# A hybrid decoder step on one core: order of the first loads, place of the tables, rows of tiles 1 to 3 ahead of the queries' weights, and the maximum of those weights on DVE

## The chip, the core and the metric

The kernel runs on one core of a Trainium2 chip. The metric is the device time of one execution in microseconds, the median of several. The core's engines each work through their own instructions in order: PE (matrix products, with PEld for loading the stationary operand), DVE (vector), ACT (activation), POOL (general), and SP, whose queue issues nearly all DMAs here. They wait for each other through semaphores.

## What is computed

One step of a one-layer decoder for 2048 prompt rows and 64 sample rows (8 sequences of 8 new tokens):

```python
h = rmsnorm(x, norm_w)
z = h @ w_in                                   # 1024 -> 3600 columns
q, k, v, qb, kb, vb, g_lr, gate_a, gate_b = jnp.split(z, split_points(), axis=-1)
q = rope(rmsnorm(heads(q, H_A), q_norm_w), pos)
k = rope(rmsnorm(heads(k, H_A), k_norm_w), pos)
o_a = attend(q, k, v)                          # mixture of three dilated windows
o_b, s_fin = gla_chunked(qb * DK_B**-0.5, kb, vb, log_a, s0)
o_b = rmsnorm(o_b, gla_norm_w)
mixed = concat([o_a * silu(gate_a), o_b * silu(gate_b)])
y = x + mixed @ w_out
```

The attention mixes windows of 128, 512 and 2048 rows with strides of 1, 4 and 16. The sample rows attend to cached keys and values in the same way. The outputs are y for prompt and sample, the last keys and values, and the states of the linear attention.

## The kernel before

**Numbers as pairs.** Every fp32 operand of the large products is split into two fp16 parts, a high one and what it leaves, after scaling by a power of two; a product is then three fp16 products (high by high, high by low, low by high). ACT writes the high part, DVE the low one. This holds for the rows x and for the weights.

**Rows.** The 2048 prompt rows are 16 tiles of 128; the sample rows are a tile of 64, called "s". `fetch` (L490) loads a tile of x, `prep` (L505) treats it: a sum of squares on ACT (L520), an inverse root in small steps on ACT and DVE (`rsqrt`, L117), the scaled high part on ACT (L528), the low part on DVE (L529), then a transposing DMA on SP (L532) into `hl`, and a store of `hl` to `h_d` (L536) for later projections. The sample tile is transposed on PE instead (L543). Tiles 0 to 3 have buffers of their own (`early`, `early_ht`).

**Weights.** `load_w` (L579) is a generator for one block of columns (v, q, k and others): eight DMAs of 128 x 512 into `raws` (L591), a maximum over the block, a scale from it, and eight splits into fp16 parts (ACT L635, DVE L636). The pool of raw buffers, `wr`, has four pairs, just one block, so the next block's loads wait until splits have released pairs. For v the maximum is exact: DVE reduces the absolute values row by row (L603). For the others ACT sums squares (L608), and two more ACT steps take the root of the largest sum (L622, L623). In both ways `spread_max` (L566) has PE turn the column of maxima (L569), DVE reduce it (L571) and PE spread the result to all partitions (L572). The scale of the columns is then `ns` (L630).

**Projections.** `project` (L1085) multiplies one tile by one block: 24 matmuls for a full tile (L1105), 16 for the sample tile (L779), into one of two PSUM buffers (`ps_Y`). `post` (L708) takes the result out: for v, ACT writes the fp32 values to a staging buffer of which there are two (L736, tag "z2"), stored by SP (L737, for the sample tile also L739), then ACT and DVE write the fp16 parts (L744, L745). For q and k, `qk_take` and `qk_post` normalize and rotate on ACT, POOL and DVE.

**Order.** The program text gives priorities, and a planner, which runs a simulated timeline, decides the order of the instructions on each engine and in SP's queue before anything runs. On the chip every engine and SP's queue keep that order, also where the first of them has to wait. The text begins (L995 to L999) with the load of the sample tile, the whole of `load_w("v")`, in which x of tile 0 goes between the fourth and the fifth load and tiles 1 to 3 behind the eighth, and then `prep` of the sample tile and tiles 0 to 3. There follow small tables: `nwo`, four loads of single columns (L1004), the attention masks `m3w` and `m3c`, the norm tables `tabs` with their power-of-two scales `scl` (L1017 to L1044). Then `first(0)` (L1124) projects v for "s" and tiles 0 to 3, q for 0 to 3, k for 0 to 3; `load_w("q")` is called behind v of tile 0, `load_w("k")` behind v of tile 3. `first(1)` to `first(3)` treat four tiles each, woven with attention work. `sample_keys` (L956) loads cached keys for the sample rows' scores; its loads need no result of the program.

## Time and profile before

| | |
|---|---|
| median of three runs | 1355.9 us (1350.35, 1355.9, 1356.49) |
| profiled execution | 1347.42 us, its span 1345.6 us |
| mean granted clock of PE | 0.979 |
| DMA | 285.27 MB, mean 212 GB/s |
| first matmul of v, tile 0 | 25.46 us |
| first matmul of q, tile 0 | 59.59 us |
| first matmul of k, tile 0 | 85.19 us |

Times in the profile count from the start of the span. A row of the timeline has the start, the length, the engine, the line of the kernel, the operation and its operands, and how many instructions were merged; in brackets stands the time for which the engine had been idle, and what ended that wait. "SPq" is SP's queue of DMA issues; the length there is that of the issue and not of the transfer. A row of the view by lines groups all instructions of a line with the same operands: busy time and mean length of one, then the idle time ahead of them.

### The profile page before, as it was taken

What the parts mean: (1) busy time and instruction counts of PE and PEld (TensorE: products, weight loads), DVE (VectorE), ACT (ScalarE), POOL (GpSimd) and SP (SyncE); (2) the same over time, 40 slices, a digit from 0 to 9 for tenths busy, and PEclk for the clock granted to TensorE, in tenths of its full rate; (3) what the DMA queues carried; (4) which work ended last, traced back from release to release, by engine and by line L of the source; (5) the groups of instructions that cost most, each with busy time, mean ns of one, the idle gap of its engine ahead of it and who ended that gap; (6) DMA issues with size and microseconds to landing.
All of it is one profiled execution on the core that took longest, in us unless ns stands there. A gap on an engine that the chain in (4) does not pass through costs nothing.

```text
span 1345.6 us, 26148 instructions
## 1 busy us (share of the span) xinstructions
PE 1218.3 (91%) x8878; PEld 722.5 (54%) x8878; DVE 933.1 (69%) x2266; ACT 878.8 (65%) x2331; POOL 641.6 (48%) x597
## 2 busy tenths in 40 slices
PE   3798999988899798998999998789999999999998
PEld 1343565555566555665766565556655544444443
DVE  6367767788677968767771769977564387787842
ACT  5655787778568877788994557655776475465520
POOL 0076554878678645651115756777440033332310
PEclk9999999999999999999999998989999999999999
DMA  8859857778957599969886355455335768998952
GB/s 259 243 162 260 233 162 161 203 203 216 238 167 207 174 278 274 299 183 220 215 190 196 85 165 199 144 168 157 98 111 190 275 197 302 376 325 312 351 200 83
DMA packets 251721, 285.27 MB, mean 212 GB/s; under 512 B 125426, under 2 KB 160195, under 8 KB 251587
## 3 DMA queue, kind: packets, MB, share of 16 engines
q1 hardware_dynamic: 251586, 283.60, 70.7%
q8 instruction: 70, 1.15, 0.4%
q14 instruction: 65, 0.52, 0.1%
HBM read 183.12 MB, written 75.24 MB: 192 GB/s over the span
## 4 chain that ended last, share of the span: by engine, by line
PE 35%; DVE 20%; DMA 17%; POOL 10%; issue 9%; ACT 6%; SPq 3%; POOLq 0%; DVEq 0%; ACTq 0%
PE Y L1579 5%; DVE qbd L243 3%; PE acc_vb L1105 3%; PE acc_qkb L1105 3%; POOL pr L951 3%; PE acc_gb L1105 3%; PE O L467 2%; PE acc_g L1105 2%; PE s L434 2%; PE t L452 2%; DMA v<-vp_d 2%; DMA qb<-q_d 2%; PE acc_q L1105 2%; PE acc_k L1105 2%; POOL pt L419 2%
## 5 line engine op out<-in xcount | busy, mean ns | idle before, releaser
L1105 PEld LDWEIGHTS <-hr 128*128 128x128 f16 x1824 | 174.5, 99 | 133.1 <-issue 21.6
L951 POOL TENSOR_TENSOR pr<-k,qb 128x512 f32<-128x512 f32 x128 | 176.5, 1379 | 115.8 <-DVE sck L952 79.7
L445 ACT ACTIVATE p<-p,o 128x256 f32<-128x256 f32 (+1 forms) x384 | 173.2, 455 | 53.3 <-DVE o L442 49.4
L1105 PEld LDWEIGHTS <-hl 128*128 128x128 f16 x1248 | 122.4, 100 | 152.3 <-issue 26.2
L1579 PE MATMUL Y<-w_o,mh 128*128 128x512 f16 x768 | 177.5, 381 | 3.5 <-ACT mh L1538 3.4
L419 POOL TENSOR_TENSOR pt<-p,pt 128x512 f16<-128x512 f32 (+1 forms) x80 | 94.4, 1180 | 145.7 <-ACT pt L418 126.1
L1621 POOL TENSOR_TENSOR tc<-oc,w 128x512 f32<-128x512 f32 x32 | 49.0, 1550 | 178.7 <-DVE w L1613 169.5
L467 PE MATMUL O<-v,pt 128*128 128x128 f16 x1200 | 110.3, 220 | 25.1 <-DMA v<-vp_d 7.9
L1579 PEld LDWEIGHTS <-mh 128*128 128x128 f16 x768 | 71.9, 98 | 91.4 <-issue 8.8
L952 DVE TENSOR_REDUCE sck<-pr 128x8 f32<-128x512 f32 x128 | 87.0, 680 | 48.9 <-POOL pr L951 48.5
L452 PE MATMUL t<-ident,p 128*128 128x128 f32 x600 | 105.4, 279 | 5.0 <-ACT p L445 3.0
L467 PEld LDWEIGHTS <-pt 128*128 128x128 f16 x1200 | 81.9, 98 | 51.8 <-POOL pt L419 12.0
L1105 PE MATMUL acc_v<-w_v,hl 128*128 128x512 f16 x384 | 95.2, 391 | 8.5 <-DVE vp L745 3.5
L442 DVE CUSTOM_DVE_ANT_0 p<-s,m3w,scl_s 128x128 f32<-128x128 f32 (+1 forms) x256 | 89.0, 394 | 17.2 <-POOL pt L419 6.0
L1105 PE MATMUL acc_g<-w_g,hr 128*128 128x272 f16 (+1 forms) x768 | 99.2, 277 | 0.0
L1105 PE MATMUL acc_vb<-w_vb,hr 128*128 128x512 f16 x384 | 96.3, 397 | 1.4 <-ACT zg L719 1.4
L1105 PE MATMUL acc_q<-w_q,hl 128*128 128x512 f16 x384 | 93.1, 392 | 4.1 <-ACT zs_k L663 3.4
L235 ACT ACTIVATE E<-D_e 128x256 f32<-128x256 f32 (+1 forms) x168 | 67.8, 418 | 44.4 <-DVE qbd L243 16.9
L1105 PE MATMUL acc_k<-w_k,hl 128*128 128x512 f16 x384 | 91.2, 383 | 2.1 <-ACT zs_k L663 1.6
L1105 PE MATMUL acc_gb<-w_gb,hr 128*128 128x512 f16 x384 | 88.4, 385 | 3.0 <-ACT zgb L728 3.0
L434 PE MATMUL s<-kk,qq 128*128 128x256 f16 (+1 forms) x512 | 79.6, 269 | 9.5 <-DMA kk<-kp_d 4.8
L227 POOL TENSOR_TENSOR D_e<-b_e 128x512 f32<-128x512 f32 x56 | 66.4, 1196 | 23.2 <-ACT E L235 11.0
(508 smaller groups left out, 2598.2 us busy)
## 6 DMA issues: line engine op xcount, KB each, us to landing
k<-in_cache_k_win SPq DMA_DIRECT2D x104, 256.0 KB
sv<-in_cache_v_win SPq DMA_DIRECT2D x24, 1024.0 KB
hr<-h_d SPq DMA_DIRECT2D x44, 512.0 KB
qb<-q_d SPq DMA_DIRECT2D x64, 256.0 KB
o_d<-o SPq DMA_DIRECT2D x96, 132.0 KB
oc<-o_d SPq DMA_DIRECT2D x48, 264.0 KB
x<-in_x_prompt SPq DMA_DIRECT2D x16, 512.0 KB
h_d<-hl SPq DMA_DIRECT2D x16, 512.0 KB
```

Of the source, the lines that this page charges most:

```text
L227: POOL.tensor_tensor(dv, bv, bv[:, :, 0:1, B - 1 : B].to_broadcast([P, M, 2, B]), ALU.subtract)
L235: ACT.activation(ev[rows, i], dv[rows, :, half, :], AF.Exp, scale=(2 * half - 1) / 16.0)
L419: POOL.tensor_tensor(l, f, h, ALU.subtract)
L434: PE.matmul(s_ps[:, i * w : (i + 1) * w], q, k, start=(n == 0), stop=(n == len(prods) - 1),)
L442: DVE.tensor_tensor_reduce(s[:, sl], s_ps[:, sl], mask, neg, BIG, ALU.add, ALU.min, nmf(i))
L445: ACT.activation(s[:, sl], s[:, sl], AF.Exp, bias=nmf(i), scale=-1.0, accum_out=denf(i))
L452: PE.transpose(p_ps[:, i * P : (i + 1) * P], t["s"][:, i * P : (i + 1) * P], ident[:])
L467: PE.matmul(o_, t["pt"][:, c, (i * nb + b) * P : (i * nb + b + 1) * P], vf(i, b), start=(n == 0), stop=(n == 2 * nb - 1),)
L951: POOL.tensor_tensor(pr[:], kt, qt, ALU.mult)
L952: DVE.tensor_reduce(out, pr[:].rearrange("p (u k d) -> p u k d", u=2, k=4), AX.X, ALU.add)
L1105: PE.matmul(z, a_[:, k, :], w[:, p_, k, cols], start=(k == 0 and i == 0), stop=(k == KT - 1 and i == 2),)
L1579: PE.matmul(Y[:], a_[:, k, :], w_[:, part, k, :512], start=(i == 0), stop=(i == len(prods) - 1),)
```

## The change

A context `tc.issue_after(i)` gives every instruction written inside it that runs on the engine of `i` an edge, so that the planner puts it behind `i` on that engine. It is no wait: an engine's own order is all it sets. For a DMA the engine is SP. The change notes some instructions (the two parts of a tile's rows, `last["ht"]`; a tile's transposing DMA; a block's last raw load and last split) and uses them so:

- All eight loads of v's weights go ahead of x of tiles 0 to 3.
- In the text v's maximum and scale come first, then the sample tile and tile 0, then two of v's eight splits, then the other six, behind the two parts of tile 0.
- Tile 1 is treated behind v's last split, tiles 2 and 3 behind the parts of tile 1, on ACT and DVE alike.
- The arithmetic on masks and norm tables goes behind the parts of tile 3 on ACT and DVE; their loads have no edge. The loads of `nwo` move to a place behind `first(1)`, and behind k's raw loads.
- The projections of v for "s" and tile 0 do their ACT and DVE work behind the parts of tile 2.
- The loads of q's weights go behind the transposing DMA of tile 0; DVE's work on them goes behind its part of tile 2. Their maximum is taken in the exact way, by DVE.
- The loads of cached keys go behind k's raw loads.

```diff
@@ prep
-                ACT.activation(as_x(ht[:, 0]), x, AF.Copy, scale=rs[:])
-                DVE.scalar_tensor_tensor(
-                    as_x(ht[:, 1]), x, rs[:], as_x(ht[:, 0]), ALU.mult, ALU.subtract
-                )
-                SP.dma_start_transpose(
+                last["ht"] = (
+                    ACT.activation(as_x(ht[:, 0]), x, AF.Copy, scale=rs[:]).ins,
+                    DVE.scalar_tensor_tensor(
+                        as_x(ht[:, 1]), x, rs[:], as_x(ht[:, 0]), ALU.mult, ALU.subtract
+                    ).ins,
+                )
+                last["turned"] = SP.dma_start_transpose(
                     hl[:].rearrange("p a k c -> p (a k) c"), ht.rearrange("p a c -> p (a c)")
-                )
+                ).ins
@@ load_w
-                SP.dma_start(raw[:, :n], src[k * P : (k + 1) * P, c0 : c0 + n])
+                last["raw"] = SP.dma_start(raw[:, :n], src[k * P : (k + 1) * P, c0 : c0 + n]).ins
...
-            exact = name == "v"
+            exact = name in ("v", "q")
...
+                last["w"] = (
+                    ACT.activation(h, raws[k][:, :n], AF.Copy, scale=nws[:, k : k + 1]).ins,
+                    DVE.scalar_tensor_tensor(
+                        l, raws[k][:, :n], nws[:, k : k + 1], h, ALU.mult, ALU.subtract
+                    ).ins,
                 )
@@ scores_of
-                    sample_keys(*todo[i])
+                    with tc.issue_after(last["raw_k"]):
+                        sample_keys(*todo[i])
@@ the start
-        at_once(load_w("v", [0], [1, 2, 3]))
+        parts = load_w("v", (), [0, 1, 2, 3])
+        for _ in range(KT + 1):
+            next(parts)
         prep("s")
-        for t in range(4):
-            prep(t)
+        prep(0)
+        for _ in range(2):
+            next(parts)
+        with ExitStack() as rows0:
+            for i_ in last["ht"]:
+                rows0.enter_context(tc.issue_after(i_))
+            at_once(parts)
+        turned0 = last["turned"]
+        with ExitStack() as split_v:
+            for i_ in last["w"]:
+                split_v.enter_context(tc.issue_after(i_))
+            prep(1)
+        with ExitStack() as split_v:
+            for i_ in last["ht"]:
+                split_v.enter_context(tc.issue_after(i_))
+            prep(2)
+            ht2 = last["ht"]
+            prep(3)
...
+        tables = ExitStack()
+        for part_ in last["ht"]:
+            tables.enter_context(tc.issue_after(part_))
         m3c = at1.tile([P, 384], F32, name="m3c")
...
         DVE.reciprocal(unq[:], scl["q"][:])
+        tables.close()
@@ first, m == 0
-                        yield from project(name, [t])
+                        with ExitStack() as rows2:
+                            if name == "v" and t in ("s", 0):
+                                for i_ in ht2:
+                                    rows2.enter_context(tc.issue_after(i_))
+                            yield from project(name, [t])
                         if name == "v":
                             if t == 0:
-                                at_once(load_w("q"))
+                                with ExitStack() as order:
+                                    order.enter_context(tc.issue_after(turned0))
+                                    order.enter_context(tc.issue_after(ht2[1]))
+                                    at_once(load_w("q"))
                             elif t == 3:
                                 at_once(load_w("k", (), [4, 5, 6]))
+                                last["raw_k"] = last["raw"]
@@ first, m == 1
+                with tc.issue_after(last["raw_k"]):
+                    output_rows()
```

`output_rows` holds the memset of `nwo` and its four loads, unchanged.

More of the change, by code (lines that the diff above doesn't have):

```diff
@@ L575, in spread_max @@
             return pt[:, P : P + 1]
-        loaded, powers = {}, {}
+        loaded, powers, last = {}, {}, {}
         def load_w(name, between=(), behind=()):
@@ L634, in load_w @@
                 h, l = w[:, 0, k, :n], w[:, 1, k, :n]
-                ACT.activation(h, raws[k][:, :n], AF.Copy, scale=nws[:, k : k + 1])
-                DVE.scalar_tensor_tensor(
-                    l, raws[k][:, :n], nws[:, k : k + 1], h, ALU.mult, ALU.subtract
+                last["w"] = (
[3 more added lines that the diff above has]
+                    ).ins,
                 )
@@ L1028, in tile_hymba @@
                 )
+        for nm_ in "qk":
+            i = "qk".index(nm_)
+            w = tabs[:, 0, i]
             pw = scl[nm_]
```

7 lines of the change are left out of this document (4 added, 3 removed).

## The prediction

> **What bounds the kernel now.** The page first: which engine fills the span, and where it does not.
>
> ```profile
> span 1345.6 us, 26148 instructions
> PE 1218.3 (91%) x8878; PEld 722.5 (54%) x8878; DVE 933.1 (69%) x2266; ACT 878.8 (65%) x2331; POOL 641.6 (48%) x597
> PE   3798999988899798998999998789999999999998
> ```
>
> PE is busy for 91% of the span, and its row lacks most in the first slices of 33.6 us each. A table by stretches puts numbers on that (columns: length, then busy time and instructions of PE, PEld, DVE, ACT, POOL, granted clock, DMA share, GB/s).
>
> ```profile
> 0.00:25.00 25.00, 3.78 (x14) 1.88 (x14) 14.08 (x54) 16.36 (x34) 1.98 (x8) 1.00 0.75 232
> 25.00:60.00 35.00, 28.80 (x114) 12.09 (x115) 17.93 (x38) 19.15 (x40) 0.95 (x1) 0.95 0.91 266
> 60.00:110.00 50.00, 44.21 (x194) 19.23 (x193) 29.62 (x49) 30.60 (x67) 33.90 (x54) 0.97 0.64 192
> 400.00:1345.60 945.60, 875.60 (x6754) 530.82 (x6752) 658.01 (x1588) 604.13 (x1597) 416.74 (x350) 0.98 0.69 213
> ```
>
> PE loses 21 us before 25 us and 6 us in each of the next two stretches. The change touches only what runs there, so the question is when PE gets through the first projections. The timeline of PE has the marks (start, length, then in brackets the idle time before and what ended it).
>
> ```profile
> 25.46 1.89 PE L1105 MATMUL acc_v<-w_v,hl 128*128 128x512 f16 x4 [0.92 <-DMA hl<-early_ht]
> 38.15 5.35 PE L1105 MATMUL acc_v<-w_v,hl 128*128 128x512 f16 x24 [2.22 <-DMA hl<-early_ht]
> 52.73 7.03 PE L1105 MATMUL acc_v<-w_v,hl 128*128 128x512 f16 x24 [3.52 <-DVE vp L745]
> 59.59 5.34 PE L1105 MATMUL acc_q<-w_q,hl 128*128 128x512 f16 x24
> 67.55 6.38 PE L1105 MATMUL acc_q<-w_q,hl 128*128 128x512 f16 x21 [0.74 <-DVE vp L745]
> 85.19 5.34 PE L1105 MATMUL acc_k<-w_k,hl 128*128 128x512 f16 x24
> 110.41 5.34 PE L1105 MATMUL acc_v<-w_v,hl 128*128 128x512 f16 x24 [1.87 <-ACT zs_k L663]
> ```
>
> The values' projection of tile 0 starts at 25.46, tile 1 at 38.15, tile 3 at 52.73; the queries start at 59.59, the keys at 85.19. A full tile is 24 matmuls in 5.34. I follow one mark, the queries' start at 59.59: what is won up to there is won for good if the later work keeps its distances.
>
> **What holds the front.** The same view of ACT, DVE and SP's queue, with DVE's scaling of v's weights:
>
> ```profile
> 9.52 2.35 SPq L1004 DMA_DIRECT2D nwo<-in_gla_norm_w  x4
> 9.52 1.06 ACT L520 ACTIVATE jk<-x 128x1024 bf16<-128x1024 f32 x1 [2.25 <-DMA x<-in_x_prompt]
> 12.36 0.68 DVE L603 TENSOR_REDUCE wm_v<-wr_v 128x1 f32<-128x512 f32 x1
> 13.27 0.16 DVE L616 TENSOR_REDUCE w_v<-wm_v 128x1 f32<-128x8 f32 x1
> 14.37 1.28 DVE L529 SCALAR_TENSOR_TENSOR early_ht<-x,rs,early_ht 128x1024 f16<-128x1024 f32 x1 [0.20 <-ACT early_ht L528]
> 16.47 0.23 DVE L630 TENSOR_SCALAR ns_v<-nw,pr_v 128x8 f32<-128x8 f32 x1
> 18.85 0.43 SPq L961 DMA_DIRECT2D k<-in_cache_k_win  x1
> 19.55 3.85 SPq L532 DMA_TRANSPOSE hl<-early_ht  x1
> 21.79 0.22 DVE L1030 TENSOR_REDUCE scl_k<-tabs 128x1 f32<-128x64 f32 x1 [3.94 <-DMA tabs<-in_k_norm_w]
> 26.34 0.16 DVE L1044 RECIPROCAL unq<-scl_q 128x1 f32<-128x1 f32 x1
> 26.41 2.92 DVE L636 SCALAR_TENSOR_TENSOR w_v<-wr_v,ns_v,w_v 128x512 f16<-128x512 f32 x4
> 31.69 6.67 SPq L532 DMA_TRANSPOSE hl<-early_ht  x2
> 39.09 3.63 SPq L532 DMA_TRANSPOSE hl<-early_ht  x1
> 46.14 0.33 SPq L536 DMA_DIRECT2D h_d<-hl  x1
> 46.52 0.46 SPq L739 DMA_DIRECT2D v_d<-vs_s  x1
> 49.88 0.69 ACT L736 ACTIVATE vs<-acc_v,wi_v 128x512 f32<-128x512 f32 x1 [8.63 <-DMA v_d<-vs_s]
> ```
>
> Three things are late. DVE stands for 3.94 us on a table that nothing near needs, with v's weights behind it; they end at 29.33 though their scale was there at 16.70. Tile 0's rows are done at 15.65 (14.37 + 1.28), but SP issues their transposing DMA only at 19.55, after table and cache loads, and PE sees it at 25.46, 5.9 later. The three other transposes go out at 31.69 to 42.7; the last is in when SP moves on at 46.14. Behind it stands the store of the sample's values (46.52), whose staging buffer ACT needs back: 8.63 us of ACT, and tile 3 waits.
>
> **The sum, step by step.**
>
> Loads. Eight weight loads now go ahead of x0. The weights' last maximum ended at 13.04 (12.36 + 0.68); without half a megabyte of x0 in their midst I take 12.0, and their scale 14.8: the chain from 13.27 to 16.70 took 3.4, of which about 0.6 was the 1.28 us L529 in its way. x0 lands later: the last four weight loads, 1 MB that now goes ahead of it, came in between x0 (9.52) and the start of the last maximum (12.36), at most 2.8 us for them; so 12.2 and not 9.52. Tile 0's rows took 6.1 us from landing to last part (9.52 to 15.65), about 1 of it behind v's maxima; so 17.5, which is 1.9 **later** than before. Bounds: 16.5 to 18.5.
>
> Queue. The cache loads wait for k's weights, and the four loads of L1004 (2.35 us of SP at 9.52) move behind them; SP is free when tile 0 is ready. Its transpose goes out at 17.5 instead of 19.55 and lands at 23.4 with the same 5.9: 2.1 won. The loads of q and k norm tables are held by nothing in the diff, only their arithmetic is; I count them as hidden, under the wait for tile 0. Without that cover they cost up to the 2.1.
>
> Weights of v. DVE does eight of 0.73 from 17.5 on at the latest: 23.3 instead of 29.33. The 3.94 goes, and the sixteen small table operations go behind tile 3; two of them stand above with 0.22 and 0.16 us, the last ending at 26.50, so I estimate 2.8 us for all.
>
> Rows of tiles 1 to 3. They now start only behind v's last split, on ACT and on DVE, where they ran ahead in gaps before. Without its square (1.06 and its readout) and the 1 us behind maxima, tile 0's chain took 3.8 of its 6.1; from 23.3 that gives 27.1 for tile 1. Tile 2 takes the same 3.8 with tile 3's square in its way: 32.1; tile 3 33.4. Transposes: tile 1 goes out at 27.2 and takes the 6.5 seen before (31.69 to 38.15): 33.7, 4.4 earlier. SP needs 3.6 for each, so tile 3's goes at 35.7 and lands, with the 7.0 of before (39.09 to 46.1), at 42.7.
>
> PE. Tile 0 and sample rows took 10.5 us (25.46 to 38.15 less the wait of 2.22): from 23.4 to 33.9. Tile 1 then runs to 39.2, tile 2 to 44.5. The new wait: ACT and DVE free the first two PSUM buffers only behind tile 2's rows (32.1), a microsecond ahead of 33.9. Queued behind that wait are, on ACT, both tiles' evictions, on DVE those and q's maxima, and PE waits for them from its third accumulator on. Tile 3 needs tile 1's accumulator, and so the staging buffer again: if that store still queues behind the last transpose, 42.7 + 0.4 + 3.25 (46.52 to landing) + 2.0 for ACT, ACT, DVE gives 48.3; if it slips in between, 44.5. Between these I take 45.7, under the middle, since the store itself needs SP for only 0.46; tile 3 ends at 51: **8.6 us won** at the queries' mark.
>
> Weights of q. The groups of the view by lines, then the chain:
>
> ```profile
> L603 DVE TENSOR_REDUCE wm_v<-wr_v 128x1 f32<-128x512 f32 x8 | 5.4, 676 | 3.4 <-DMA wr_v<-in_w_in 3.4
> L608 ACT ACTIVATE jw_q<-wr_q,nw 128x512 bf16<-128x512 f32 x8 | 5.7, 710 | 6.2 <-DMA wr_q<-in_w_in 6.2
> L608 ACT ACTIVATION_READ_ACCUMULATOR jw_q<-wr_q,nw 128x1 f32 x8 | 1.5, 189 | 0.0
> L745 DVE SCALAR_TENSOR_TENSOR vp<-acc_v,vp 128x512 f16<-128x512 f32 x4 | 2.8, 690 | 2.4 <-ACT vp L744 2.4
> 39.46 0.16 DVE L616 TENSOR_REDUCE w_q<-wm_q 128x1 f32<-128x8 f32 x1 [1.44 <-ACT jw_q L608]
> 43.34 0.27 PE L569 MATMUL mx_q<-ident,w_q 128*1 128x128 f32 x1
> 48.08 0.38 PE L572 MATMUL mx_q<-mm_q,ident 1*128 1x1 f32 x2
> 51.37 0.23 DVE L630 TENSOR_SCALAR ns_q<-nw,pr_q 128x8 f32<-128x8 f32 x1
> 52.59 5.39 DVE L636 SCALAR_TENSOR_TENSOR w_q<-wr_q,ns_q,w_q 128x512 f16<-128x512 f32 x8
> 81.92 3.39 DVE L636 SCALAR_TENSOR_TENSOR w_k<-wr_k,ns_k,w_k 128x512 f16<-128x512 f32 x5
> ```
>
> ACT loses 7.2 us of squares (5.7 + 1.5) and two small steps; DVE gains 5.4. But DVE starts them behind tile 2's rows. From 32.1 it has tile 3 (1.28), tables (2.8), the evictions of sample, tile 0 and tile 1 (about 0.7 each) and the maxima (5.4): 43.6, later than the 39.46 of before. The chain to the scale took 12.1 then (39.46 to 51.60), 7.9 of it waiting for PE's turn twice; of the last 3.1 (48.46 to 51.60) I estimate that 2.0 go with the two ACT steps, since v's whole chain took 3.4 with an empty PE. So the scale comes between 43.6 + 3.4 = 47.0 and 43.6 + 10.1 = 53.7; PE has a gap near 44.5 in the plan above, so I take 48, near the lower end. Splits need 6.4 to the last (51.60 to 57.98): 54.4, and a query tile that starts at 51 ends at 56.3, not held.
>
> The keys. Their loads need q's raw buffers, so they come 3.6 earlier (57.98 to 54.4), their last split at 81.7 instead of 85.31, and the first key tile ends by 82.4 at best; by PE's own pace (51 + 25.6 + 5.3) 81.9. Before it ended at 90.53. So 8.1 to 8.6 are kept: **8.4**. Beyond, tables, cache loads and L1004's loads are needed tens of microseconds later and cost nothing; if the planner orders later work anew, I allow 4 either way.
>
> The profiled execution took 1347.42 (span 1345.6 and 1.8 around it): 1339.0. It lies 8.5 under the median of the three runs; from the median, 1355.9 - 8.4 = **1347.5**.
>
> Tile 3's 7.03 behind a pause of 3.52, against 5.34 elsewhere, prices a cold restart at 1.7. The Trainium skill (TensorE: Matmul & The Clock Gate, "Why this matters for your kernels") says that pauses over about 3 us between bursts drop the clock; the trace agrees. Should tile 0 end by 30 and tile 1 not be in before 33.7, that rule would make it 1349.2.
>
> **The rivals.**
>
> *More is won.* The 2.6 us before 67.55 arise because the last eviction of values stands behind k's squares; and from 59.59 to 110.41 eight tiles of 42.7 take 50.8. With the store slipped in (start at 49.8, 9.8 won) and half of those 8.1 gone: 13.8, so 1342. For it: ACT has 7 us less to do. Against: k keeps its squares, and POOL's share (33.9 of 50) does not move.
>
> *DVE becomes the bound.* If both PE turns in q's chain come as late as before, the scale is there at 53.7; the first query tile ends at 60.8 (64.93 before), k's splits are 2.1 later than before (87.4), the first key tile ends at 88.1: 2.4 won, 1353. For it: every step is in DVE's order behind tile 2. The skill (VectorE: DVE Perf Modes, "Rules for kernel authors") advises against `tensor_reduce` on a hot path as the slowest operation there; the trace has 676 ns against ACT's 710 + 189, so it doesn't bear out slowness for one, only the place in the queue.
>
> *Slower: the strict order of rows.* If v's weights don't come earlier (29.3 as now) and tiles 1 and 2 each take the 6.1 of tile 0 in series, tile 2 is done at 41.5; then 11.5 of DVE and the old chain without ACT give q's scale at 53 + 10.1 = 63.1, 11.5 later than before; k's last split follows at 96.8 and the first key tile at 97.5, 7 late: 1363. It decides from the point at which tile 2's rows end behind 36.5, where tile 1 would have started anyway. Against it: the 3.94 is seen to go.
>
> *The change doesn't do what it says.* The table loads stay ahead on SP's queue, tile 0's transpose goes out at 19.6 again and its landing paces all: 1356.
>
> **How the numbers follow.** A measurement of this kernel tells about 0.5%, 6.8 us, from no change. Forecast 0.38 (own range 1344 to 1352; three quarters of it under 1349.1), more won 0.24, DVE the bound 0.21, nothing 0.03, slower 0.14. Faster: 0.28 + 0.24 = 0.52; same: 0.10 + 0.21 + 0.03 = 0.34; slower 0.14. The range 1338 to 1358 holds all but the slower case and the tip of the large gain.
>
> **What would show it.** Right: no wait of DVE on a table before v's splits; their end near 23; tile 0's transpose out near 17.5 and PE on it near 23.4; tile 1 near 34; queries near 51, first key tile ended near 82; the distance from there to the end unchanged. Wrong: tile 2's rows behind 36.5, PE waiting on evictions before tile 1, q's scale later than 51, or a key stretch that starts early and ends at the old time.

## The result and the profile after

The changed kernel takes 1359.66 us (median of 20, 1354.27 to 1365.18) against 1352.52 of the kernel before (20, 1344.09 to 1358.37). The ratio is 1.0053 with a 95% interval of 1.0039 to 1.0067: **slower by half a per cent**, where a gain of 8.4 us was forecast. The time is above the range of 1338 to 1358. The profiled execution took 1359.95; the one of before, 1347.42, lies 5.1 under its median, so marks of the two traces differ at the end by 12.6, of which the medians confirm 7.1.

Of the page of the changed kernel, the span, the engines and PE's row by slices:

```profile
span 1358.2 us, 26126 instructions
PE 1221.8 (90%) x8878; PEld 725.9 (53%) x8878; DVE 939.4 (69%) x2275; ACT 872.3 (64%) x2313; POOL 637.1 (47%) x597
PE   3877999889899797998889898799999999899998
```

PE's work is the same within 0.3%; its second to fourth slices read 8, 7, 7 where they read 7, 9, 8 before. The table by stretches (columns as before):

```profile
0.00:25.00 25.00, 8.52 (x30) 3.73 (x31) 16.71 (x45) 12.90 (x25) 1.97 (x8) 1.00 0.81 252
25.00:60.00 35.00, 27.00 (x115) 11.55 (x114) 19.55 (x55) 16.03 (x27) 0.45 (x1) 0.90 0.80 218
60.00:110.00 50.00, 36.77 (x159) 15.66 (x157) 28.32 (x49) 30.07 (x68) 28.01 (x51) 0.95 0.68 195
400.00:1358.20 958.20, 885.57 (x6807) 537.91 (x6805) 664.59 (x1597) 608.92 (x1611) 424.64 (x356) 0.98 0.68 211
```

Up to 25 us PE does 4.7 us more than before (8.52 against 3.78). From 25 to 60 it does 1.8 less, from 60 to 110 it does 7.4 less (36.77 against 44.21), and POOL 5.9 less. So the gain was there at first and is lost in the stretches of the queries and keys. PE's timeline has the marks:

```profile
22.82 3.17 PE L1137 MATMUL acc_v<-w_v,hl 128*128 128x512 f16 x13
...
36.24 8.20 PE L1137 MATMUL acc_v<-w_v,hl 128*128 128x512 f16 x28 [6.36 <-DVE za L789]
44.28 0.27 PE L571 MATMUL mx_q<-ident,w_q 128*1 128x128 f32 x1
...
48.80 0.38 PE L574 MATMUL mx_q<-mm_q,ident 1*128 1x1 f32 x2
...
55.88 0.39 PE L1137 MATMUL acc_q<-w_q,hl 128*128 128x512 f16 x1 [0.61 <-DVE vp L749]
...
86.52 5.34 PE L1137 MATMUL acc_k<-w_k,hl 128*128 128x512 f16 x24 [2.71 <-ACT zs_q L667]
...
109.08 6.77 PE L1137 MATMUL acc_k<-w_k,hl 128*128 128x512 f16 x24 [3.93 <-ACT zs_k L667]
116.54 5.34 PE L1137 MATMUL acc_v<-w_v,hl 128*128 128x512 f16 x24 [0.70 <-ACT zs_k L667]
127.04 8.01 PE L1137 MATMUL acc_q<-w_q,hl 128*128 128x512 f16 x24 [5.16 <-ACT zs_k L667]
```

Tile 0 starts 2.6 us earlier, the queries 3.7 (55.88 against 59.59), the keys already 1.3 **later** (86.52 against 85.19), v's tile 4 later by 6.1 (116.54 against 110.41). What stands behind the first losses is in the timelines of DVE, ACT and SP's queue:

```profile
15.03 0.23 DVE L632 TENSOR_SCALAR ns_v<-nw,pr_v 128x8 f32<-128x8 f32 x1
16.64 1.75 DVE L530 SCALAR_TENSOR_TENSOR early_ht<-x,rs,early_ht 128x1024 f16<-128x1024 f32 x1 [0.61 <-ACT early_ht L529]
18.32 5.38 DVE L639 SCALAR_TENSOR_TENSOR w_v<-wr_v,ns_v,w_v 128x512 f16<-128x512 f32 x8
18.42 1.94 SPq L534 DMA_TRANSPOSE hl<-early_ht  x1
30.75 1.28 DVE L530 SCALAR_TENSOR_TENSOR early_ht<-x,rs,early_ht 128x1024 f16<-128x1024 f32 x1 [0.84 <-ACT early_ht L529]
31.95 3.64 DVE L605 TENSOR_REDUCE wm_q<-wr_q 128x1 f32<-128x512 f32 x6
35.51 0.67 DVE L789 TENSOR_TENSOR za<-za,acc_v_s 64x512 f32<-64x512 f32 x1
39.81 0.14 DVE L618 TENSOR_REDUCE w_q<-wm_q 128x1 f32<-128x8 f32 x1
41.23 3.61 SPq L534 DMA_TRANSPOSE hl<-early_ht  x1
44.90 0.58 SPq L750 DMA_DIRECT2D vp_d<-vp  x1
48.56 0.60 ACT L748 ACTIVATE vp<-acc_v 128x512 f16<-128x512 f32 x1 [4.21 <-DMA vp_d<-vp]
50.43 0.23 DVE L632 TENSOR_SCALAR ns_q<-nw,pr_q 128x8 f32<-128x8 f32 x1
54.51 0.60 ACT L748 ACTIVATE vp<-acc_v 128x512 f16<-128x512 f32 x1 [4.77 <-DMA vp_d<-vp]
55.00 5.00 ACT L638 ACTIVATE w_q<-wr_q,ns_q 128x512 f16<-128x512 f32 x8
```

Tile 2's rows end at 32.03, as forecast. Then DVE takes six of q's maxima (3.6 us) before the sample's addition `za` (35.51), which frees the first accumulator: PE waits 6.36 us. Some 3.5 of these would have been there anyway, since tile 1's rows land only at 33.39; the other 2.9 are the wait for `za`. The column of q's maxima is there at 39.95, but the scale only at 50.66, since its two steps on PE stand behind v's tiles 1 and 2 (44.28, 48.80). And `vp` (v's fp16 parts), which has one buffer, waits for its store, which stands behind tile 3's transposing DMA on SP (41.23, 44.90).

### The profile page after: what moved, and what is told of

Read it like the earlier page. It is cut to its first block, busy times and chain, and to the rows that moved or that the text cites. A ratio compares the mean times of both kernels' runs of the same rounds, so it can differ in the third digit from the quotient of the medians.

```text
span 1358.2 us, 26126 instructions
## 1 busy us (share of the span) xinstructions
PE 1221.8 (90%) x8878; PEld 725.9 (53%) x8878; DVE 939.4 (69%) x2275; ACT 872.3 (64%) x2313; POOL 637.1 (47%) x597
## 4 chain that ended last, share of the span: by engine, by line
PE 39%; DVE 20%; DMA 14%; issue 10%; POOL 10%; ACT 5%; SPq 2%; POOLq 0%; DVEq 0%; ACTq 0%
PE Y L1621 7%; PE acc_vb L1137 4%; PE acc_qkb L1137 3%; DVE qbd L243 3%; PE acc_g L1137 3%; POOL pr L955 3%; PE acc_gb L1137 3%; PE O L467 2%; DMA qb<-q_d 2%; PE t L452 2%; DMA T_q<-qp_d 2%; PE s L434 2%; POOL pt L419 2%; PE acc_q L1137 2%; DVE p L442 2%
## 5 line engine op out<-in xcount | busy, mean ns | idle before, releaser
L467 PE MATMUL O<-v,pt 128*128 128x128 f16 x1200 | 111.3, 222 | 29.4 <-POOL pt L419 9.4
L467 PEld LDWEIGHTS <-pt 128*128 128x128 f16 x1200 | 82.9, 99 | 55.9 <-POOL pt L419 14.1
L1137 PE MATMUL acc_q<-w_q,hl 128*128 128x512 f16 x384 | 95.9, 399 | 7.8 <-ACT zs_k L667 5.2
L227 POOL TENSOR_TENSOR D_e<-b_e 128x512 f32<-128x512 f32 x56 | 66.4, 1195 | 23.3 <-ACT E L235 11.0
```

The costliest lines, as they stand in the source:

```text
L227: POOL.tensor_tensor(dv, bv, bv[:, :, 0:1, B - 1 : B].to_broadcast([P, M, 2, B]), ALU.subtract)
L467: PE.matmul(o_, t["pt"][:, c, (i * nb + b) * P : (i * nb + b + 1) * P], vf(i, b), start=(n == 0), stop=(n == 2 * nb - 1),)
L1137: PE.matmul(z, a_[:, k, :], w[:, p_, k, cols], start=(k == 0 and i == 0), stop=(k == KT - 1 and i == 2),)
```

## The experiments

The theories, in the order in which they came. **A**: `vp`'s store holds q's splits and, through them, all that follows. **C**: the moved loads (L1004's four, cached keys) collide with k's. **B**: the gain of the front is given back in the key stage, where the planner orders the engines differently; its rival **H**: that stage is long whatever the order. Two marks carry the summary: in the kernels below, POOL rotates q's and k's tiles 0 to 3 one after another (L687 and L693 before, L691 and L697 after), and "first" and "eighth rotation" are the starts of the first and last of these eight, from POOL's timeline. A row of the table tells its kernel apart from the kernel before where its interval leaves out 1.

| kernel | ratio to before, 95% | first | eighth | between |
|---|---|---|---|---|
| before | 1 | 68.07 | 121.58 | 53.5 |
| changed | 1.0053, 1.0039 to 1.0067 | 71.46 | 129.04 | 57.6 |
| a_vp2 | 1.0066, 1.0042 to 1.0090 | 72.99 | 128.85 | 55.9 |
| a_evict_first | 1.0046, 1.0028 to 1.0064 | 73.21 | 130.63 | 57.4 |
| a_loads_back | 1.0066, 1.0047 to 1.0084 | 73.43 | 129.89 | 56.5 |
| a_free_evict | 1.0033, 1.0017 to 1.0049 | 67.82 | 123.72 | 55.9 |
| a_free_rot | 1.0033, 1.0015 to 1.0052 | 69.13 | 124.99 | 55.9 |
| a_q_on_act | 1.0012, 0.9995 to 1.0030 | 70.22 | 123.15 | 52.9 |
| b_moved | 1.0019, 0.9999 to 1.0038 | 66.78 | 127.58 | 60.8 |
| b_exact | 1.0041, 1.0020 to 1.0061 | 73.33 | 127.37 | 54.0 |
| a_free_q_act | 0.9976, 0.9953 to 0.9998 | 64.39 | 118.62 | 54.2 |
| a_both_pins | 1.0054, 1.0034 to 1.0075 | 71.88 | 128.73 | 56.9 |
| b_zs_half | 1.0028, 1.0003 to 1.0053 | 68.51 | 122.14 | 53.6 |
| a_zs_half | 1.0108, 1.0073 to 1.0142 | 71.64 | 126.92 | 55.3 |
| a_scale_first | 1.0036, 1.0013 to 1.0059 | 70.24 | 129.31 | 59.1 |
| b_scale_first | 1.0020, 0.9996 to 1.0043 | 70.53 | 122.29 | 51.8 |
| a_keys_store | 1.0039, 1.0020 to 1.0059 | 71.99 | 124.99 | 53.0 |
| a_scale_keys | 1.0033, 1.0010 to 1.0055 | 70.25 | 128.42 | 58.2 |
| b_scale_vp2 | 1.0003, 0.9984 to 1.0022 | 67.87 | 119.29 | 51.4 |
| a_free_q_act_vp2 | 0.9971, 0.9954 to 0.9987 | 63.73 | 119.41 | 55.7 |

Names with a_ start from the changed kernel, with b_ from the kernel before. Some expectations go by another mark, the stretch on PE from k's tile 0 to q's tile 4. It took 33.9 us before, 40.5 in the changed kernel, 41.0 in a_evict_first, 39.6 in a_free_evict, 41.3 in a_free_rot, 35.8 in a_q_on_act, 36.9 in a_free_q_act, 40.5 in a_both_pins, 43.9 in b_moved, 38.7 in b_exact and 43.7 in a_zs_half.

**One wait or one group of loads at a time.** Two buffers for `vp` (a_vp2); the first rows of the next tiles behind q's and k's evictions on ACT (a_evict_first); the moved loads put back (a_loads_back).

```diff
-tag="vp", bufs=1)                                   # a_vp2
+tag="vp", bufs=2)
+if t in (4, 5, 6, 7):                               # a_evict_first
+    taken.enter_context(tc.issue_after(last["zs"]))
 high = ACT.activation(as_x(ht[:, 0]), x, AF.Copy, scale=rs[:]).ins
-with tc.issue_after(last["raw_k"]):                 # a_loads_back
-    sample_keys(*todo[i])
+sample_keys(*todo[i])
...
+output_rows()
```

> The changed kernel with two buffers instead of one for the fp16 parts of v (tag vp). Theory A (in the changed kernel ACT stands 4.77 us in front of the queries' splits because the store of v's parts has not left its only buffer; the splits start at 55.00 instead of 50.7, and this delay runs on through the keys' weights): the wait goes, the first q split starts near 50.7, w_k's last split ends near 85 instead of 89.5, tile 4's q starts near 122 instead of 127.0, and the time falls by about 4 us, to a ratio of 1.002 against the kernel before. Theory B (the planner's order on ACT in the key stage: the rows' part of tiles 4 and 5 ahead of the evictions of keys 0 and 1): q starts earlier, but tile 4's q stays within 2 us of 127 and the ratio stays near 1.005. Theory C (the loads moved behind k's raw loads are in the way): as B.

> The changed kernel with one more edge: ACT's high part of the rows of tiles 4 to 7 is put behind the eviction of the latest key tile, as the kernel before has it for tiles 4 to 6. Theory B: PE's waits on key evictions ahead of key tiles 2 and 3 and of q of tile 4 (1.87, 3.93, 5.16 us) fall to those of before (0.6, 1.0, 3.4), tile 4's q starts near 121 to 122 instead of 127.0, and the ratio falls from 1.005 to about 1.001. Theory A: the stage is late from w_k on, the waits only change places, tile 4's q stays above 125, ratio 1.004 to 1.006.

> The changed kernel with the loads of cached keys free again and the four single-column loads of nwo back at their old place in the text, ahead of the masks. Theory C (four nwo loads of 3.1 us of SP at 64.6 and four cache loads up to 76.7 stand among w_k's and v's loads and delay the rope tables, x of tiles 4 to 6 and the stores): x of tile 4 is issued near 82 instead of 85.3, the key stage loses less, ratio near 1.002. Theories A and B: the first loads lose about 2 us at the start again and the key stage keeps its waits; ratio 1.005 to 1.008.

None of the three brings the time back. With two buffers ACT's waits for the store are gone and q's splits begin at 51.13 instead of 55.00, yet q's tile 0 starts at 55.31 and k's at 88.06. SP's queue in a_vp2 shows why:

```profile
55.56 0.57 SPq L849 DMA_DIRECT2D v<-vp_d  x1
57.21 1.21 SPq L593 DMA_DIRECT2D wr_k<-in_w_in  x2
```

The store of `vp` goes out at 50.98. The load that reads it back (L849) waits for it in SP's queue until 55.56, and k's loads stand behind that: they go out at 57.21, as in the changed kernel (57.19). So ACT's wait for the buffer falls as the whole cause. The store itself isn't cleared by this run: the wait for it only moved from ACT to SP's queue, and the early splits brought k's loads nothing.

With the loads back the first rotation is at 73.43 and the ratio 1.0066: C falls. The order on ACT alone leaves the key stage as long as it was (57.4).

**Undoing the two parts that touch q's scale.** Without the holds on the evictions of the sample and tile 0 (a_free_evict), with q's maximum from ACT's squares again (a_q_on_act), and both (a_free_q_act).

```diff
-if name == "v" and t in ("s", 0):      # a_free_evict
+if False:
-exact = name in ("v", "q")             # a_q_on_act
+exact = name == "v"
```

> The changed kernel without the edges that hold the v projections of the sample tile and tile 0 behind tile 2's rows on ACT and DVE. In the changed kernel PE stands 6.36 us before tile 1 (29.9 to 36.24) for DVE's addition of the sample accumulator, which follows six maxima of q. Without the edges this wait should end when tile 1's rows have landed, near 33.4. Theory A and B alike: q does not start earlier than 54, since its splits wait for the same vp store on ACT; the ratio stays within 0.002 of 1.005. If instead the time falls by 3 us or more, the hold on evictions is itself the loss.

> The changed kernel with the queries' weights scaled as before, by ACT's squares instead of DVE's maxima. Its listing has, unlike the changed kernel's, each key eviction ahead of the next rows' high part on ACT and most rotations ahead of the next tile's small steps on POOL, as the kernel before. Theory B2 (the loss lies in the order that the planner gives ACT and POOL from the first key tile to q of tile 4: 40.5 us there in the changed kernel against 33.9 before): that distance returns to 34 to 36 and the ratio is 0.999 to 1.002, whatever the maxima cost. Theory D (DVE's maxima are a gain or a loss of their own in the front): the distance stays near 40, q starts 2 us or more later than 55.9 and the ratio is above 1.006, or q starts earlier and it falls.

> The changed kernel with two of its parts undone together: the sample's and tile 0's evictions aren't held, and q's maximum is taken from ACT's squares again (what is left: the loads in the order of need, the tables behind the rows, the rows ahead of q's maximum). Theory B (the front's gain is given back in the key stage because the planner orders ACT and POOL differently there when q's weights come early): the order in the listing is that of before, so the first key tile starts at 82 to 85 and the stretch from there to q's tile 4 takes 34 to 36 (before 33.9, changed 40.5); q's tile 4 at 117 to 120; ratio 0.997 to 1.000. Rival H (the stretch is long whenever the key tiles begin early, whatever the order: what it waits for isn't moved with it): k0 at 82, the stretch 39 to 41, q's tile 4 at 121 to 123, ratio 1.002 to 1.004.

| ratio to before | q's maximum on DVE | on ACT |
|---|---|---|
| evictions held | 1.0053 | 1.0012 |
| evictions free | 1.0033 | 0.9976 |

DVE's maximum costs 0.41% with the holds and 0.57% without, where the intervals lie apart; the holds cost 0.20% and 0.36%, where the intervals overlap. The maximum does not cost it the same way twice: with the holds q's scale is even later without it (51.86 against 50.66), and most of the gain is in the length of the chain of rotations (52.9 against 57.6); without the holds most of it is in the chain's start (64.39 against 67.82). With both undone, what is left of the change (loads, tables, rows ahead) is **faster** than the kernel before: 0.9976, interval below 1. How, the timelines of a_free_q_act show:

```profile
40.73 0.38 PE L574 MATMUL mx_q<-mm_q,ident 1*128 1x1 f32 x2 [0.37 <-DVE mm_q L573]
43.31 5.01 ACT L638 ACTIVATE w_q<-wr_q,ns_q 128x512 f16<-128x512 f32 x8 [1.04 <-DVE ns_q L632]
50.24 1.27 SPq L593 DMA_DIRECT2D wr_k<-in_w_in  x2
63.57 0.68 ACT L667 ACTIVATE zs_q<-acc_q,wi_q 128x512 f32<-128x512 f32 x1
64.39 1.27 POOL L691 TENSOR_TENSOR t_q<-zs_q,ct_q 128x512 f32<-128x512 f32 x1 [21.23 <-ACT zs_q L667]
```

PE takes q's two steps in its gap ahead of tile 2. The scale is there at 43.3, splits release raw buffers, k's loads go out at 50.24 (57.19 in the changed kernel), k's eight squares, which stand on ACT ahead of q's first eviction, are through at 61.48 instead of 70.16, and POOL's rotations begin at 64.39 instead of 71.46. What ACT waits for last is then PE's first query tile, which ends at 62.9. In a_free_evict PE is as early, but DVE's maxima give their column at 42.2 and the second PE step comes at 52.47; splits at 53.79.

**The same parts put into the kernel before.** Only the eight moved loads (b_moved), only DVE's maximum (b_exact).

```diff
+with tc.issue_after(last["raw_k"]):    # b_moved, also around output_rows()
     sample_keys(*todo[i])
-exact = name == "v"                    # b_exact
+exact = name in ("v", "q")
```

> The kernel before with only the cached keys' loads and nwo's loads moved behind k's raw loads. Its listing has the changed kernel's order on ACT (rows' part ahead of the evictions of keys 0 and 1) and POOL in the key stage. Theory B2: the first loads and tile 0's transpose go out 2 to 4 us earlier, but the distance from the first key tile to q of tile 4 rises from 33.9 to 39 to 41; ratio 1.000 to 1.004. Against it: the distance stays near 34 and the ratio falls to 0.997 or less.

> The kernel before with only the queries' maximum taken by DVE. Its listing keeps the order of the kernel before in the key stage. Theory B2: the distance from the first key tile to q of tile 4 stays at 33 to 36; the scale of q comes earlier by ACT's two steps and their waits, q starts 0 to 3 us earlier; ratio 0.997 to 1.000. Theory D as a loss: q starts later than 59.6, ratio above 1.002.

DVE's maximum alone costs 0.41% here too: PE waits 9.06 us for `vp` ahead of v's tile 3, and the rotations begin 5.3 later, though k's loads go out at 54.30, as before (54.04). So here the harm does not come through q's scale. b_moved starts the rotations 1.3 earlier and ends them 6.0 later. Eight small loads moved out of the way were enough to make the key stage 7 us longer; its time comes out level (1.0019).

**Forcing the order of the key stage.** POOL's root steps behind the rotation of the tile before (a_free_rot, without the holds), and that with ACT's order of a_evict_first (a_both_pins).

```diff
+if "rot" in last and t in (0, 1, 2, 3):
+    turn.enter_context(tc.issue_after(last["rot"]))
 rsqrt(sm, rs[:n, : g * NH], ss[:n, : g * NH], 1.0 / HD, n, g * NH, tag, eng=POOL)
```

> The kernel with free evictions (ratio 1.0033) with one more edge: for tiles 0 to 3 POOL's small steps of the inverse root stand behind the rotation of the tile before, as in the kernel before. Theory B2, if POOL's order carries it: the distance from the first key tile to q of tile 4 falls from 39.6 to 36 or less, and the ratio to 0.999 to 1.001. If it is ACT's order, or the evictions themselves, the distance stays at 39 to 41 and the ratio at 1.002 to 1.005.

> The changed kernel with two edges added that force the order of the kernel before in the key stage on both engines at once: on ACT the high part of the rows of tiles 4 to 7 behind the latest eviction zs, on POOL the small steps of a tile's root behind the last rotation of the tile before. One of them at a time left the stretch k0 to q4 at 41.0 and 41.3. Theory B: both together bring it to 34 to 36, ratio 1.000 to 1.002. Rival H: it stays at 39 to 42 (k0 near 87), ratio 1.004 to 1.007.

Both miss: 55.9 and 56.9 between the rotations, no change in time. So the longer stage is not the order on ACT and POOL that these edges force. SP's queue was left. POOL and SP's queue in the changed kernel:

```profile
101.93 1.27 POOL L691 TENSOR_TENSOR t_k<-zs_k,ct_k 128x512 f32<-128x512 f32 x1 [0.71 <-DVE t_q L703]
102.76 2.04 SPq L534 DMA_TRANSPOSE hl<-ht  x1
104.86 1.03 SPq L775 DMA_DIRECT2D qp_d<-qp  x1
105.94 0.57 SPq L501 DMA_DIRECT2D x<-in_x_prompt  x1
107.28 0.34 SPq L538 DMA_DIRECT2D h_d<-hl  x1
107.67 2.04 SPq L815 DMA_TRANSPOSE qq<-qp_d  x1
109.81 0.53 SPq L760 DMA_DIRECT2D out_k_win_prompt<-t_k  x1
114.37 1.40 POOL L697 TENSOR_TENSOR t_k<-zs_k,ct_k 128x256 f32<-128x256 f32 x2 [2.00 <-DMA out_k_win_prompt<-t_k]
```

and in the kernel before:

```profile
101.21 2.35 SPq L532 DMA_TRANSPOSE hl<-ht  x1
104.04 0.34 SPq L756 DMA_DIRECT2D out_k_win_prompt<-t_k  x1
104.43 0.57 SPq L501 DMA_DIRECT2D x<-in_x_prompt  x1
```

Before, the store of the rotated keys goes out 2.8 us behind the rows' transposing DMA and ahead of the next fetch. In the changed kernel it stands behind a store, a fetch, another store and another transposing DMA, 7.1 us; POOL needs its buffer back and waits, then ACT's eviction waits for POOL and PE for ACT. Between the first and the eighth rotation POOL waits 3.6 us for this store, 0.2 before; the chain is 4.1 longer. Among the kernels up to here this store is 6.8 to 8.6 us behind wherever the chain takes more than 55 us (a_vp2 6.8, a_free_evict 7.4, b_moved 7.4, a_both_pins 7.2), and 1.9 to 2.4 in a_q_on_act, a_free_q_act and b_exact, where it takes less.

**SP's order, and q's scale on PE.** From here on theory R: the time follows the chain of POOL's rotations, its start q's scale, its length the keys' store. The store of keys ahead of the next fetch and rows (a_keys_store); v's tile 2 behind the second PE step of q's maximum (a_scale_first, b_scale_first); both (a_scale_keys).

```diff
+with tc.issue_after(last["ko"]):                    # a_keys_store; h_d's store too
     fetch(t + 7)
+if name == "v" and t == 2:                          # a_, b_scale_first
+    rows2.enter_context(tc.issue_after(last["q"]))  # b_: order.enter_context
 yield from project(name, [t])
```

> The changed kernel with edges on SP alone: the fetch of the next row tile and the store of the rows just turned stand behind the store of the rotated keys of tiles 0 to 3, as they do in the kernel before. Theory R: the first rotation stays at 71 to 72, the store of tile 0's keys goes out within 3 us of the first turning of rows (7.1 us in the changed kernel, 2.8 before), POOL no longer waits for it (5.2 us between 80 and 135), the first to the eighth rotation takes 54 to 55.5 (57.6), ratio 1.001 to 1.004. Rival (the store is late because the keys are late, not because of SP's order): the chain stays at 57 to 58, ratio 1.004 to 1.007.

> The changed kernel with one edge: v's tile 2 on PE stands behind the second PE step of q's maximum, so that q's scale doesn't wait for 20 matmuls of that tile. Theory R (the time follows POOL's chain of eight rotations, and its start follows q's scale): q's scale ends at 45 to 47 (50.7 in the changed kernel), w_k's first raw load goes out at 52 to 54 (57.19), the first rotation is at 66 to 68 (71.46), the eighth at 123 to 125 (129.04), ratio 1.000 to 1.003. Rival Z (what is late is decided on the way from the key stage to the end, by an order planned anew): the scale and the first rotation come earlier as said, the ratio stays at 1.004 to 1.007. Rival Y (w_k's loads wait for something else than w_q's splits): the scale is early, the first rotation stays at 70 to 72.

> The kernel before with the same edge and nothing of the change. Theory R: q's scale at 46 to 48 (51.6 before), w_k's first raw load at 49 to 51 (54.04), the first rotation at 64 to 66 (68.07), the eighth at 117.5 to 120 (121.58), ratio 0.996 to 0.999: most of what the change was to bring, by one edge. Rival Z: the first rotation as early, ratio 0.999 to 1.003.

> The changed kernel with both edges, on PE for q's scale and on SP for the keys' stores. Theory R: first rotation 66 to 68, eighth 120 to 123, ratio 0.998 to 1.001. Rival Z: eighth rotation as early, ratio 1.003 or more.

a_keys_store does in the main what R says in the trace: the store goes out at 107.04, 4.4 us behind the rows' transposing DMA (within 3 was expected), POOL's waits for it nearly go, and the chain takes 53.0, even less than expected. The view of waits from 80 to 135 us (total, times, longest) of the changed kernel

```profile
POOL t_k L697 <- DMA out_k_win_prompt<-t_k: 5.2, 3, 2.0
```

and of a_keys_store:

```profile
POOL t_k L700 <- DMA out_k_win_prompt<-t_k: 0.9, 1, 0.9
```

The time, 1.0039, is in R's span, but its interval overlaps that of the changed kernel. So the cause of the longer stretch in the changed kernel is shown, and H, by which no order would shorten it, falls; its 4 us in the trace are not shown to be 4 in the time.

The earlier scale fails. In a_scale_first PE does its step at 43.64, but DVE has the next steps behind `vp`'s low part, and the scale comes at 50.94 (50.66 in the changed kernel). In b_scale_first the splits do start at 45.68 (51.84 before) and k's loads at 47.88 (54.04), but the first rotation is 2.5 later. PE and ACT there:

```profile
52.52 5.34 PE L1105 MATMUL acc_v<-w_v,hl 128*128 128x512 f16 x24 [2.96 <-DVE vp L745]
62.35 3.38 PE L1105 MATMUL acc_q<-w_q,hl 128*128 128x512 f16 x9 [4.49 <-DVE vp L745]
69.12 0.69 ACT L662 ACTIVATE sq_q<-acc_q,wi_q 128x512 f32<-128x512 f32 x1 [3.08 <-PE acc_q L1105]
```

PE waits for `vp`, the buffer of A, which holds q's tile 0 also when the scale is early. So q's start has two limits side by side, which the next kernel was to take away together. The edge doesn't add to a_keys_store either: a_scale_keys has 58.2 between the rotations, and 1.0033. There POOL never waits for the keys' store in the chain, but 4.65 us for the rows on ACT and 4.08 for k's splits on DVE; in b_scale_first it waits 3.96 for the store and has one of the shortest chains, 51.8. So the store's place explains the changed kernel's chain and is no rule for the others.

```diff
-tag="vp", bufs=1)          # b_scale_vp2, a_free_q_act_vp2
+tag="vp", bufs=2)
```

> The kernel before with two edits: v's tile 2 on PE behind the second PE step of q's maximum, and two buffers for vp. Theory V (q's start is held by two things side by side, the scale behind PE's tile and vp's one buffer, so that one alone brings nothing): no wait of PE for vp's store, q's tile 0 starts at 54 to 57 (59.59 before, 62.35 with the first edit alone), the first rotation at 62 to 65 (68.07 and 70.53), the eighth at 115 to 119 (121.58), ratio 0.995 to 0.999. Rival (a third thing holds q's first eviction on ACT, such as w_k's squares ahead of it): q's tile 0 at 54 to 57, the first rotation at 67 to 70, ratio 0.999 to 1.003.

> The changed kernel without the holds on v's first evictions and with q's maximum from ACT's squares, and with two buffers for vp. In the version with one buffer PE's wait ahead of v's tile 2 was for the rows' transposing DMA (3.92 us), none for vp's store; so theory V expects nothing more: q's tile 0 at 56.5 to 58 (57.54), first rotation 63 to 66 (64.39), ratio 0.996 to 0.999. Rival: 0.993 to 0.996 if vp's buffer also holds the stage behind, or 1.000 and more if the gain of the first version was an order of the plan that falls with any edit.

In b_scale_vp2 the wait ahead of q's tile 0 is gone, the one ahead of v's tile 3 is not (2.97 us for `vp`'s low part), q's tile 0 starts at 58.00, later than expected, and a third limit follows, as its rival said, though at another place than ACT: the step of **k's** maximum stands within q's tile 0 on PE.

```profile
58.00 2.11 PE L1105 MATMUL acc_q<-w_q,hl 128*128 128x512 f16 x9
62.86 0.27 PE L569 MATMUL mx_k<-ident,w_k 128*1 128x128 f32 x1 [2.75 <-DVE w_k L616]
```

The first rotation stays at 67.87, and the time is that of before (1.0003). a_free_q_act_vp2 comes out as the version with one buffer did: 0.9971, interval 0.9954 to 0.9987, median 1346.94 against 1350.64. So what is left of the change is, in two variants, faster than the kernel before by about 0.3%. Its chain takes 55.7 all the same, with the keys' store only 2.5 behind.

**The buffer between ACT and POOL.** Evicted q and k tiles use the two halves of `zs` in turn, so that an eviction no longer waits for the rotation before it.

```diff
+h_ = t % 2 if t in (0, 1, 2, 3) else i
-ACT.activation(zs[:n, i], z, AF.Copy, scale=inv[:n])
+ACT.activation(zs[:n, h_], z, AF.Copy, scale=inv[:n])
```

> The kernel before with one thing changed: the evicted q and k of tiles 0 to 3 use the two halves of the buffer zs in turn (each fills only one half there), so that a tile's eviction no longer waits for POOL's rotation of the tile before. If the loop eviction, rotation, eviction sets the pace of the key stage (a part of theory B): the stretch k0 to q4 falls from 33.9 to 29 to 32, ratio 0.996 to 0.999. Rival H (another resource: the rows' transposing DMAs, the rotations' own rate on POOL): the stretch stays at 33 to 35, the wait moves to POOL or to the rows, ratio 0.999 to 1.002.

> The changed kernel with the same two halves of zs. If the longer stretch (40.5 against 33.9) comes from evictions that wait for POOL's late rotations: the stretch falls to 33 to 36 and the ratio to the kernel before to 0.999 to 1.002. Rival H: it stays at 38 to 42, with the wait at another place, ratio 1.004 to 1.007.

In b_zs_half PE goes from k's tile 0 (85.29) to q's tile 4 (114.69) in 29.4 us, as expected; the time is 0.28% worse, not better. PE had run ahead of a chain that kept its pace: 53.6 between the rotations. That explains why nothing was won; why something was lost is not shown. In a_zs_half ACT puts evictions ahead of rows, the rows are turned 14 us later, and PE meets that. Its SP queue and PE:

```profile
116.72 1.96 SPq L534 DMA_TRANSPOSE hl<-ht  x1
121.02 2.31 PE L1141 MATMUL acc_v<-w_v,hl 128*128 128x512 f16 x5 [7.98 <-DMA hl<-ht]
```

That is the slowest of all, 1.0108.

**Over all twenty kernels** the ratio goes with the eighth rotation (correlation 0.76) and with the first (0.80). Without the two of `zs`, whose buffer lets the rows move instead, the eighth gives 0.88 and 0.82 us of time per us, the first 0.89; that they are left out was decided after they had run. Scatter of 0.1 to 0.2% remains, as wide as the intervals, and each mark is from one execution. A correlation does not show that the chain sets the time: that is argued from the waits, and the edit that was meant to shorten it alone, a_keys_store, did not change the time beyond its interval.

## Why the prediction was wrong

**Held.** v's scale was forecast for 14.8 (measured 15.26, the end of its row at 15.03), tile 0's rows for 17.5 (18.39), the DMA out at 17.5 (18.42) and PE on it at 23.4 (22.82), v's splits' end at 23.3 (23.70). The 3.94 us of DVE went. Tile 1's rows came at 27.57 for 27.1, tile 2's at 32.03 for 32.1, tile 1's landing by 33.39 for 33.7. DVE waited for no table ahead of the splits. (The terms given for tile 0's rows, 12.2 + 6.1 - 1, add up to 17.3 and not 17.5; nothing hangs on it.) The rival of a strict order of rows, with tile 2 behind 36.5, did not come about, though the change came out slower.

**First failure: "Tile 3 ends at 51: 8.6 us won".** PE's tile 1 was to start at 33.9 and started at 36.24. The plan let the evictions of the sample and tile 0 go a microsecond ahead of it, at 32.1, and counted q's maxima *behind* them on DVE. DVE had six of them in front of `za`. That is the named sign "PE waiting on evictions before tile 1". The pause also made PE cold: its granted clock was 0.50 from 36.2 to 40.0, and 28 matmuls took 8.20, where 28 at the pace of 24 in 5.34 are 6.23. Tile 3's rows ended at 38.57, not 33.4, since all eight maxima and `za` stood ahead of them on DVE; their DMA went out at 41.23, not 35.7, behind four stores on SP. 3.7 were won at the queries instead of 8.6.

**Second: "I take 48" for q's scale.** It was 50.66, in the bounds of 47.0 to 53.7; a size that was off, with the right mechanism, since the column was there 3.7 sooner than worked out (39.95 against 43.6) and from there to the second PE step 8.9 went by, 8.3 of them waiting for PE's turns. The splits, forecast right behind the scale with a last one at 54.4, started at 55.00 only, behind ACT's `vp`: that wait was priced for tile 3, not for q's splits, which stand behind it on ACT.

**Third, the step that turns the sign: "by PE's own pace" for the keys, and "the distance from there to the end unchanged".** The first key tile was to end at 82.4; it ended at 91.86. The chain that sets this stretch is not PE's. It is POOL's eight rotations with one buffer on each side, `zs` before and the store of keys behind. Its first link comes from k's squares, which stand on ACT ahead of q's first eviction:

```profile
69.36 0.72 ACT L610 ACTIVATE jw_k<-wr_k,nw 128x512 bf16<-128x512 f32 x1 [0.35 <-DMA wr_k<-in_w_in]
70.08 0.67 ACT L666 ACTIVATE sq_q<-acc_q,wi_q 128x512 f32<-128x512 f32 x1
71.46 1.27 POOL L691 TENSOR_TENSOR t_q<-zs_q,ct_q 128x512 f32<-128x512 f32 x1 [29.76 <-ACT zs_q L667]
```

Compared with before, q's splits begin 3.2 later, k's loads 3.2 later (57.19 against 54.04) and the first rotation 3.4 later: the lead of 3.7 at the queries does not reach this chain at all. The prediction saw POOL's 33.9 of 50 and took it as a load that does not move; it is a chain that moves as a whole (3.4 later) and stretches (4.1) when SP's order changes. With it PE's lead turns into 1.3 lost at k's tile 0 and 6.1 at v's tile 4. The allowance of 4 either way for a new plan was about the right size for this one stretch, but was set around a gain that was not there any more. Of the other rivals, DVE as the bound (1353) named the right part, q's maximum on DVE, which costs 0.41 to 0.57% in three pairs of kernels; but it let PE's turns be the whole harm, 6 us of the forecast's gain, where the pairs show three different ways, the chain's length, its start, and PE's wait for `vp`. That the change came out slower, to which the prediction gave 0.14, is no merit of the rival of the strict order: that had named another cause.

**Open.** Of the 12.6 us between the profiled executions 9.0 are there at q's tile 5 (145.25 against 136.22); the rest arises later and was not traced. Why the plan puts the keys' store late in some kernels and early in others isn't known either; only that it does, also when eight loads are moved. And which way DVE's maximum costs its 0.4 to 0.6% changes from kernel to kernel, so the loss is shown for that part of the change and only argued for each link of the way.

The Trainium skill (TensorE: Matmul & The Clock Gate, "Why this matters for your kernels") warns of pauses over about 3 us between bursts. The traces agree where the change made such pauses: no loss behind 1.87 us, 6.77 for a tile behind 3.93, 8.01 behind 5.16. Over all the runs the border is less sharp: in a_scale_keys a tile took 7.03 behind 2.09 us, at a granted clock of 0.51 in its first 3.4 us, and in a_free_q_act one took 5.34 behind 3.68, at a granted clock of 1.00.

## What to carry to other kernels

Where a plan fixes every queue's order, a forecast of a front-loaded change has to name the slowest chain of the *next* stage and its first link, and then ask whether the change moves that link; here, by the waits in the changed kernel's trace, it was POOL's rotation, fed by q's scale through raw buffers, k's loads and k's squares. A step of a few hundred nanoseconds on a busy in-order engine (a maximum spread over PE, a store behind a transposing DMA) can cost the whole piece of work that stands ahead of it: look at what stands before it, not at its length. Undo the parts of a change in pairs: here two of them hid what the rest had won.

## What was not expected

A cold restart had no fixed price: 1.4 us behind 3.93 us of pause (6.77 against 5.34), 2.0 behind 6.36 (8.20 against 6.23) and 2.7 behind 5.16 (8.01 against 5.34). And taking away a wait that the profile shows as PE's largest in the key stage made both kernels slower (1.0028 and 1.0108): PE had waited there for a chain that did not get faster. In the changed kernel rows turned 14 us later came on top; the loss in the kernel before has no shown cause.
